# Context and x tokens out of step in the second block of a two-block fp32 kernel

## The chip, the cores and the metric

One core of one Trainium2 chip runs the whole program. The metric is the device time of one execution in microseconds.

## What is computed

Two transformer blocks run one after the other on 256 tokens of width 1024, all in float32. The first block is attention with spatial gating and a mixture of 32 experts. The second block has two layers, in which the 256 tokens of x and 256 tokens of a context run through the same weights; the context can be read by x's attention, and the last layer needs of the context only its keys and values. Cut to what matters:

```python
def swiglu(h, w_gu, w_down):
    g, u = jnp.split(h @ w_gu, 2, axis=-1)
    return (jax.nn.silu(g) * u) @ w_down

for layer in range(2):
    last = layer == 1
    mx = jnp.split(jax.nn.silu(c) @ ada_w[layer] + ada_b[layer], 9, axis=-1)
    mc = jnp.split((jax.nn.silu(c_ctx) @ ada_w[layer] + ada_b[layer])[None, :], 9, axis=-1)
    x   = x   + 0.5 * mx[2][:, None] * swiglu(modulate(rms_norm(x),   mx[0], mx[1]), ffn1_gu, ffn1_down)
    ctx = ctx + 0.5 * mc[2][:, None] * swiglu(modulate(rms_norm(ctx), mc[0], mc[1]), ffn1_gu, ffn1_down)
    hx, hc = modulate(rms_norm(x), mx[3], mx[4]), modulate(rms_norm(ctx), mc[3], mc[4])
    # q, k, v, pool and fourier inputs = h @ w_in; x attends to x and ctx, ctx to ctx
    x = x + mx[5][:, None] * merge_mixers(ax, upx, ufx, ...)      # [attention, pool, fourier] @ w_out
    x = x + 0.5 * mx[8][:, None] * swiglu(modulate(rms_norm(x), mx[6], mx[7]), ffn2_gu, ffn2_down)
    if not last:
        ctx = ctx + mc[5][:, None] * merge_mixers(ac, upc, ufc, ...)
        ctx = ctx + 0.5 * mc[8][:, None] * swiglu(modulate(rms_norm(ctx), mc[6], mc[7]), ffn2_gu, ffn2_down)
return rms_norm(x) * final_gain
```

## The kernel before

**Precision.** Every large product is made of three matmuls (`mm3`, L116 to L118): weights and tokens are each split into a high part and the rest. A weight tile of 512 KB is loaded by SP's queue into `raw`, copied to `whi` by ScalarE (L89), and VectorE subtracts the copy to get `wlo` (L90). There are eight `raw` buffers and four each of `whi` and `wlo`.

**Order.** The code is written as one sequence of tiles, and a scheduler sets the order of the instructions on each engine when the program is built. Each engine then has its own list of instructions.

**The feed-forward** (`ffn`). The hidden width is 22 blocks of 128, taken as 11 pairs. A pair needs four weight tiles for gate and up, and 96 matmuls; in layer 0's FFN2 and layer 1's FFN1 the moving operand has 512 columns, x's 256 tokens beside ctx's 256. Pairs go in groups (0 to 4, 4 to 8, 8 to 11), and a group ends with its down-projection, whose results `gated_add` puts onto x or ctx (L890, L891). Layer 0's FFN1 of ctx is done beside the experts of the first block, ahead of all this.

**A norm** (`norm_hT`, `row_norm`) is a chain over three engines: ScalarE squares and sums a row, VectorE makes the inverse root from small operations (L135 to L146) and the normalised rows `xs` (L160), TensorE transposes them (L122), and ScalarE and VectorE put scale and shift on them and split them into `hT` (L212, L109, L110). Nothing of the next product can start before.

**The mixer** projects keys and values, queries, and the inputs of pool and fourier, for ctx and x in turn; attention, pool and fourier write a copy `cat`. Pool multiplies with a matrix `poolc` for each of four windows, loaded by POOL's queue into one buffer and used for both streams. Then the output projection goes over two halves of the columns, in each half first x's tokens, then ctx's.

**Modulation.** The rows mx and mc of layer 1 are made on VectorE while layer 0 runs: 72 steps, each a load of 512 KB into an `araw` buffer (five of them) and two products with a sum (L840, L841), against two rows of c that also lie in `araw` buffers (`c_rows`, L817). A step comes after every second weight tile (`rate`). The first steps wait, by a copy (L820), for the tile in `self.gate`, the last `hT` of the norm before layer 0's FFN2.

Of the kernel before, what the change touches and what calls it, by code (L numbers as in the profile page):

```python
# [6 lines left out]
F32 = mybir.dt.float32  # L7
# [18 lines left out]
RB = (0,0)  # L26
# [22 lines left out]
W1 = (8,4,4)  # L49
class Builder:  # L50
    def __init__(self, tc, A):
        self.tc, self.nc, self.A = tc, tc.nc, A
        self.side, self.mods = [], {}
        self.rate, self.credit, self.done = 0, 0, 0
        self.gate, self.tanh, self.part, self.turn_ = None, False, {}, 0

# [21 lines left out]
    def W(self, name, idx, cols=1024):  # L78
# [7 lines left out]
        raw = self.t(self.wp, [128, 1024], F32, "raw", self.RAW)  # L86
# [4 lines left out]
        return hi, lo  # L91

# [85 lines left out]
    def norm_hT(self, x, gcol, scol, hh, hl, off, tags=None, ahead=AH):  # L178
# [13 lines left out]
        for kp in range(4):  # L192
# [3 lines left out]
            s = (slice(None), slice(2 * kp, 2 * kp + 2), slice(off, off + 256))  # L196
            if scol is None:
                for kk in range(2):
                    kt = 2 * kp + kk
                    g = gcol[:, kt : kt + 1]  # L200
                    h, l = hh[:, kt, off : off + 256], hl[:, kt, off : off + 256]
# [26 lines left out]
    def build(self, parts=None):  # L228
        tc, nc, A = self.tc, self.nc, self.A
        self.PB = {"mm": 3, "at": 2, "tr": 2, "ada": 1}  # L230
        with tc.tile_pool(name="glob", bufs=1) as G, \
# [11 lines left out]
            with tc.tile_pool(name="keep", bufs=1, reuse_waits="tile") as K:  # L243
# [7 lines left out]
                nc.gpsimd.dma_start(kv, self.ctx)  # L251
            with tc.tile_pool(name="ctxp", bufs=1, reuse_waits="tile") as C:
# [20 lines left out]
    def proj_T(self, p, wb, c, hh, hl, ts, kts=range(8)):  # L273

        for kt in kts:
            wh, wl = wb[kt // 4]
            s = slice((kt % 4) * 256 + c * 128, (kt % 4) * 256 + c * 128 + 128)
            self.mm3(p, (wh[:, s], wl[:, s]), (hh[:, kt, ts], hl[:, kt, ts]), kt == 0, kt == 7)

    def block1(self):  # L280
        tc, nc, A = self.tc, self.nc, self.A
        x = self.x
        T256 = slice(0, 256)
        with tc.tile_pool(name="b1", bufs=1, reuse_waits="tile") as P:
# [4 lines left out]
            self.norm_hT(x, n1g, None, hh, hl, 0, ("tr", "tr", "at", "at"), 4)  # L289
# [58 lines left out]
            for g2 in range(4):  # L348
                wu = [self.W("w_u", 2 * g2 + b) for b in range(2)]
                for c in range(2):  # L350
                    pu = self.mm([128, 256])
                    self.proj_T(pu, wu, c, hh, hl, T256)
# [114 lines left out]
            def merge(br, yT):  # L467
                for d2 in range(4):
                    wg = [self.W("w_gate", br * 8 + 2 * d2 + b) for b in range(2)]
                    wu = [self.W("w_up", br * 8 + 2 * d2 + b) for b in range(2)]  # L470
                    for c in range(2):
                        d = 2 * d2 + c
                        pg = self.mm([128, 256])
                        self.proj_T(pg, wg, c, hh, hl, T256)
# [5 lines left out]
                        self.proj_T(pu, wu, c, yT[:, 0], yT[:, 1], T256)  # L480
# [22 lines left out]
            self.norm_hT(self.ctx, self.seg(mods, 1, 1), self.seg(mods, 1, 0), *self.cT, 0, ("tr",) * 4, 2)  # L503
# [13 lines left out]
    def moe(self):  # L517
        tc, nc, A = self.tc, self.nc, self.A
        x = self.x
        with tc.tile_pool(name="moe", bufs=1, reuse_waits="tile") as P:  # L520
            self.xsp, self.xst = P, ("xg", 6)
            self.gp, self.gpb = P, 1
            ctx_steps = self.ffn(P, 0, 1, ((self.ctx, 0, self.grow(self.mods[0][1], 1, 2)),), self.cT, 256, CUT)
# [129 lines left out]
            def raws(name, idx):  # L653

                out = []
                for n in idx:
                    self.turn_ = (self.turn_ + 1) % (self.RAW + 5)
                    r = self.t(self.wp, [128, 1024], F32, *(("araw", 5) if self.turn_ % 3 == 0 else ("raw", self.RAW)))
# [235 lines left out]
    def ffn(self, P, L, f, streams, hT, n, cuts, first=None):  # L894
# [4 lines left out]
        nb = 2 * max(b - a for a, b in zip(cuts, cuts[1:])) + 2  # L899
        for c0, c1 in zip(cuts, cuts[1:]):  # L900
            hid = []
            for j in range(c0, c1):
                pgu = [[self.mm([128, n], tag) for c in range(2)] for tag in ("mm", "at")]

                parts = [slice(off, off + 256) for _, off, _ in streams] if j == 0 and len(streams) > 1 else [slice(0, n)]
                parts = parts if first is None else parts[::first]
                if len(parts) > 1:
                    wb = [[self.W(gu, (L, o + 2 * j + b)) for b in range(2)] for o in (0, 22)]
                    for ts in parts:
                        for w in range(2):  # L910
                            for c in range(2):
                                self.proj_T(pgu[w][c][:, ts], wb[w], c, *hT, ts)
                else:
                    for w in range(2):
                        for b in range(2):
                            wt = self.W(gu, (L, 22 * w + 2 * j + b))
                            for c in range(2):
                                self.proj_T(pgu[w][c], [wt, wt], c, *hT, parts[0], range(4 * b, 4 * b + 4))
                for c in range(2):
                    s = self.t(P, [128, n], F32, "silu", 2)  # L920
                    fh = self.t(P, [128, n], F32R, "fh", nb)
                    fl = self.t(P, [128, n], F32R, "fl", nb)
# [13 lines left out]
            for c in range(2):  # L936
                out = [(x, off, g, tt) for x, off, g in streams for tt in range(2)]
# [9 lines left out]
                for p, (x, off, g, tt) in zip(ps, out):  # L947
                    self.gated_add(p, g, x, tt, c)
                    if c1 == cuts[-1] and c == 0 and first is not None:
                        self.half(x, tt)  # L950
# [3 lines left out]
    def mixer(self, L, mods, d2, last, hT):  # L954
        nc, tc, A = self.nc, self.tc, self.A
        x, ctx = self.x, self.ctx
        sc, sx = ("c", ctx, 256, 1), ("x", x, 0, 0)
        streams = (sx, sc) if last else (sc, sx)
        full = (sx,) if last else (sc, sx)
        for _, xx, off, a in streams if last else (sx,):  # L960
            self.norm_hT(xx, self.seg(mods, a, 4), self.seg(mods, a, 3), hT[:, 0], hT[:, 1], off)
        with tc.tile_pool(name="mix", bufs=1, reuse_waits="tile") as P:
# [30 lines left out]
            def proj(wb, ncol, stream, ev):  # L993
                kper = 8 // len(wb)
                nm, xx, off, a = stream
                for tt in range(2):
                    p = self.mm([128, ncol])
                    ts = slice(off + tt * 128, off + tt * 128 + 128)
                    for kt in range(8):
                        wh, wl = wb[kt // kper]  # L1000
                        s = slice(kt % kper * ncol, kt % kper * ncol + ncol)
                        self.mm3(p, (hT[:, 0, kt, ts], hT[:, 1, kt, ts]), (wh[:, s], wl[:, s]), kt == 0, kt == 7)
# [86 lines left out]
            cat = self.t(self.B, [128, 2, 8, 512], F32R, "hT")  # L1089

            def attention(stream):
# [3 lines left out]
                for tt in range(2):  # L1095
# [28 lines left out]
                    ts = slice(off + tt * 128, off + tt * 128 + 128)  # L1124
                    self.split(p, cat[:, 0, 0:4, ts], cat[:, 1, 0:4, ts])
# [279 lines left out]
```

## Time and profile before

| | |
|---|---|
| time, median of 3 runs | 2228.83 us (2227.14 to 2238.33) |
| profiled execution | 2229.63 us, span 2227.8 us |
| TensorE busy | 2106.4 us, 95% of the span |
| VectorE, ScalarE busy | 1298.9 us (58%), 838.4 us (38%) |
| mean clock granted to TensorE | 0.979 of full speed |
| DMA | 437.95 MB, 197 GB/s over the span |

A matmul's busy time overlaps the next one's, so busy TensorE is read by the gaps it leaves and by its clock. The second block begins at about 870 us and runs to the end.

### The profile page before, as it was taken

The page shows a single profiled execution, that of the slowest core. Times are in us where ns is not written, and L with a number is a line of the kernel's source. Part 1 is how long each engine was busy: PE and PEld are TensorE (multiplying, and loading weights), DVE is VectorE, ACT ScalarE, POOL GpSimd, SP SyncE. Part 2 cuts the span into 40 slices and gives each one's busy share as a digit, 9 for nine tenths or more (in the row PEclk, how much of TensorE's full clock was granted, in tenths as well). Part 3 has the DMA queues.
Part 4 walks back from the last instruction along what each step waited for, and adds up shares of the span by engine and source line. Part 5 has one row for each costly group of instructions (what it writes and reads, how often), then busy time and mean ns, then how long its engine had stood idle before and what let it go on. Part 6 is the DMA issues. An engine that isn't in the chain of part 4 may idle for free. (4 is left out here: it accounts for less than half of the span.)

```text
span 2227.8 us, 31222 instructions
## 1 busy us (share of the span) xinstructions
PE 2106.4 (95%) x12146; PEld 1695.5 (76%) x12146; DVE 1298.9 (58%) x2311; ACT 838.4 (38%) x1322; POOL 55.4 (2%) x105
## 2 busy tenths in 40 slices
PE   7999999999996999999989999999999999898998
PEld 5888797446464888888778888878888887677997
DVE  5778575223236455685589434998843344856655
ACT  5556453222233444455342222223222223545443
POOL 1000000000001000000000000000000000000000
PEclk9999999999997999999999999998999999899999
DMA  8655656999997867731266323665622223305552
GB/s 314 207 167 172 236 197 243 395 381 416 402 416 264 297 236 284 248 105 43 77 209 215 96 94 121 210 199 163 214 95 95 91 96 99 121 27 161 190 187 78
DMA packets 121207, 437.95 MB, mean 197 GB/s; under 512 B 14352, under 2 KB 14496, under 8 KB 120928
## 3 DMA queue, kind: packets, MB, share of 16 engines
q1 hardware_dynamic: 113760, 413.19, 52.4%
q0 software_dynamic: 7296, 22.74, 3.1%
q8 instruction: 96, 1.57, 0.3%
q14 instruction: 55, 0.45, 0.1%
HBM read 429.53 MB, written 6.34 MB: 196 GB/s over the span
## 5 line engine op out<-in xcount | busy, mean ns | idle before, releaser
L90 DVE TENSOR_TENSOR wlo<-raw,whi 128x1024 fp32r<-128x1024 f32 x448 | 546.8, 1223 | 509.7 <-ACT whi L89 502.8
L89 ACT ACTIVATE whi<-raw 128x1024 fp32r<-128x1024 f32 x448 | 473.9, 1060 | 730.8 <-PE at L117 177.9
L117 PE MATMUL mm<-hT,whi 128*128 128x256 f32 (+1 forms) x736 | 246.2, 336 | 3.1 <-DVE hT L110 2.8
L116 PE MATMUL mm<-hT,whi 128*128 128x256 f32 (+1 forms) x736 | 243.7, 337 | 3.6 <-ACT hT L109 3.6
L118 PE MATMUL mm<-hT,wlo 128*128 128x256 f32 (+1 forms) x736 | 245.1, 334 | 0.6 <-DVE wlo L90 0.6
L117 PE MATMUL at<-hT,whi 128*128 128x256 f32 (+1 forms) x736 | 244.5, 333 | 0.0
L118 PE MATMUL at<-hT,wlo 128*128 128x256 f32 (+1 forms) x736 | 243.9, 333 | 0.0
L116 PE MATMUL at<-hT,whi 128*128 128x256 f32 (+1 forms) x736 | 241.6, 333 | 0.0
L116 PE MATMUL mm<-whi,fh 128*128 128x512 f32 x440 | 172.1, 398 | 5.6 <-ACT whi L89 5.6
L117 PE MATMUL mm<-wlo,fh 128*128 128x512 f32 x440 | 175.0, 399 | 1.6 <-DVE wlo L90 1.6
L118 PE MATMUL mm<-whi,fl 128*128 128x512 f32 x440 | 173.7, 397 | 0.0
L117 PEld LDWEIGHTS mm<-hT,whi 128*128 128x128 f32 x736 | 140.8, 191 | 21.0 <-DVE hT L110 5.4
L116 PEld LDWEIGHTS mm<-hT,whi 128*128 128x128 f32 x736 | 138.9, 191 | 21.1 <-ACT hT L109 5.2
L118 PEld LDWEIGHTS mm<-hT,wlo 128*128 128x128 f32 x736 | 140.8, 191 | 16.4 <-DVE wlo L90 1.0
L117 PEld LDWEIGHTS at<-hT,whi 128*128 128x128 f32 x736 | 140.2, 191 | 16.4 <-issue 1.7
L116 PEld LDWEIGHTS at<-hT,whi 128*128 128x128 f32 x736 | 138.6, 191 | 17.2 <-ACT whi L89 1.7
L118 PEld LDWEIGHTS at<-hT,wlo 128*128 128x128 f32 x736 | 140.2, 190 | 14.7
L116 PEld LDWEIGHTS mm<-whi,fh 128*128 128x128 f32 x440 | 82.6, 189 | 32.9 <-ACT whi L89 11.2
L117 PEld LDWEIGHTS mm<-wlo,fh 128*128 128x128 f32 x440 | 82.9, 188 | 29.3 <-DVE wlo L90 4.6
L932 DVE TENSOR_TENSOR silu<-silu,at 128x256 f32<-128x256 f32 (+1 forms) x104 | 55.2, 531 | 82.4 <-PE at L118 82.1
L118 PEld LDWEIGHTS mm<-whi,fl 128*128 128x128 f32 x440 | 83.0, 189 | 19.1
L116 PE MATMUL mm<-whi,hT 128*128 128x512 f32 (+1 forms) x256 | 95.0, 377 | 2.6 <-ACT hT L109 2.5
(381 smaller groups left out, 3940.6 us busy)
## 6 DMA issues: line engine op xcount, KB each, us to landing
raw<-gu SPq DMA_DIRECT2D x220, 512.0 KB, 4.3
araw<-ada_w SPq DMA_DIRECT2D x144, 512.0 KB, 4.5
raw<-w SPq DMA_DIRECT2D x119, 512.0 KB, 10.0
raw<-dn SPq DMA_DIRECT2D x110, 512.0 KB, 4.2
araw<-w SPq DMA_DIRECT2D x73, 512.0 KB, 10.0
raw<-w_in SPq DMA_DIRECT2D x54, 512.0 KB, 4.2
raw<-w_out SPq DMA_DIRECT2D x24, 512.0 KB, 3.8
raw<-w_gate SPq DMA_DIRECT2D x16, 512.0 KB, 3.4
```

What stands on the lines that cost most here:

```text
L89: self.nc.scalar.activation(out=hi[:, :cols], in_=src, func=AF.Copy)
L90: self.nc.vector.tensor_tensor(out=lo[:, :cols], in0=src, in1=hi[:, :cols].bitcast(F32), op=OP.subtract)
L116: mm(p, lh, rh, start=first, stop=False)
L117: mm(p, lh, rl, start=False, stop=False)
L118: mm(p, ll, rh, start=False, stop=last)
L932: nc.vector.tensor_tensor(out=s, in0=s, in1=pgu[1][c], op=OP.mult)
```

## The change

In the second block the two streams no longer go through the same pairs at the same time.
- FFN2 of layer 0: pairs 0 to 3 of ctx are computed alone beside and after attention of x in the mixer; x's pairs 0 to 3 alone follow the mixer; pairs 3 to 6 and 6 to 9 take both streams; then 9 to 11 of x alone, and of ctx alone, the latter beside x's norm for layer 1.
- FFN1 of layer 1: pairs 0 to 2 of x, 2 to 6 and 6 to 9 of both, 9 to 11 of x; then 0 to 2 of ctx beside x's norm for the mixer, and 9 to 11 of ctx beside the queries of x in the mixer, then ctx's norm.
- A pair alone has matmuls of 256 columns, with tiles of its own (`lsilu`, `lfh`, `lfl`).
- In the mixer the output projection is a function per stream. In layer 0 ctx's comes before attention of x, x's at the end. Pool runs per stream, with its own loads of the matrices. In layer 1 the projection of ctx's keys and values is moved behind queries and pool/fourier inputs of x.
- `hT` is one tile for both streams that lives through the block, attention writes into it, and `cat` goes. `self.gate` is now ctx's half of it, as ctx's norm before FFN2 leaves it.
- `raw` has four buffers; in the first block and the experts four more (`rawk`) take every other load.

```diff
-W1 = (8,4,4)
+W1 = (4,4,4)
+CA = (0, 3)
+EC = (3, 6, 9, 11)
+FC = (2, 6, 9, 11)
...
+    def raw(self):
+        self.rawn += 1
+        if self.K is not None and self.rawn % 2:
+            return self.t(self.K, [128, 1024], F32, "rawk", 4)
+        return self.t(self.wp, [128, 1024], F32, "raw", self.RAW)
...
-    def ffn(self, P, L, f, streams, hT, n, cuts, first=None):
+    def ffn(self, P, L, f, parts, cuts, pre="", ends=()):
...
-        for c0, c1 in zip(cuts, cuts[1:]):
+        for streams, c0, c1 in zip(parts, cuts, cuts[1:]):
+            n = 256 * len(streams)
+            act = streams[0][2] if len(streams) == 1 else self.both
...
-            def pool():
+            def pool(stream):
+                nm, xx, off, a = stream
                 for j in range(2):
-                    ps = [self.mm([128, 256]) for _ in full]
+                    p = self.mm([128, 256])
                     for g2 in range(2):
                         g = 2 * j + g2
                         pP = self.load(P, "c_pool", [128, 2, 256], "poolc", idx=g, bufs=MC)
...
+            def out(stream):
+                nm, xx, off, a = stream
+                g = self.grow(d2, a, 5)
+                for c in range(2):
+                    ps = [self.mm([128, 512]) for _ in range(2)]
+                    for b in range(4):
+                        wh, wl = self.W("w_out2", (L, 4 * c + b))
+                        for tt, p in enumerate(ps):
...
             if last:
                 kx, kc = keys(sx), keys(sc)
                 run(proj(wkv, 256, sx, ev_kv))
                 next(kx)
-                run(proj(wkv, 256, sc, ev_kv))
+                run(proj(weights(2, 4), 512, sx, ev_q), kx)
+                run(queries(sx), side(), n=1)
+                run(proj(weights(6, 4), 512, sx, ev_pf))
+                run(proj(weights(0, 2), 256, sc, ev_kv))
                 next(kc)
-                run(proj(weights(2, 4), 512, sx, ev_q), kx)
-                run(proj(weights(6, 4), 512, sx, ev_pf), kc, queries(sx))
-                run(attention(sx), *((pool(), fourier(sx)) if ORD else (fourier(sx), pool())), n=NF)
+                run(kc, pool(sx))
+                run(attention(sx), fourier(sx), n=NF)
...
-                run(chain(attention(sc), kx, qx), proj(wpf, 512, sc, ev_pf), proj(wpf, 512, sx, ev_pf), n=NA)
-                run(attention(sx), *((pool(), fourier(sc), fourier(sx)) if ORD else (fourier(sc), fourier(sx), pool())), n=NF)
...
+                run(chain(attention(sc), kx, qx), proj(wpf, 512, sc, ev_pf), proj(wpf, 512, sx, ev_pf), pool(sc), fourier(sc), n=NA)
+                run(out(sc))
+                run(attention(sx), pool(sx), fourier(sx), side(), n=NF)
+            run(out(sx))
...
+            def alone(L, f, st, a, b, ends=()):
+                return self.ffn(B, L, f, [(st,)], (a, b), "l", ends)
...
+            def side():
+                norm(0, 1, 6)
+                cs.append(stream(0, 1, 6))
+                yield
+                yield from alone(0, 2, cs[0], *CA)
+            self.need(0, 3)
+            self.mixer(0, *self.mods[0], False, side)
+            sc, = cs
+            self.gate = T[:, 1, 1, 7].bitcast(F32)
+            self.rate = RC[0]
+            norm(0, 0, 6)
+            sx = stream(0, 0, 6)
+            ffn(0, 2, [(sx,), (sx, sc), (sx, sc), (sx,)], (0, *EC), (x,))
+            self.need(1, 1)
+            norm(1, 0, 0)
+            run(alone(0, 2, sc, *EC[-2:], (ctx,)))
+            self.rate = RA[1]
+            sx = stream(1, 0, 0)
+            norm(1, 1, 0)
+            sc = stream(1, 1, 0)
+            ffn(1, 1, [(sx,), (sx, sc), (sx, sc), (sx,)], (0, *FC), (x,))
+            self.need(1, 2)
+            norm(1, 0, 3)
+            run(alone(1, 1, sc, 0, FC[0]))
+            def side():
+                yield from alone(1, 1, sc, *FC[-2:], (ctx,))
+                norm(1, 1, 3)
+            self.mixer(1, *self.mods[1], True, side)
+            norm(1, 0, 6)
+            ffn(1, 2, [(stream(1, 0, 6),)] * 3, (0, 4, 8, 11), (x,))
```

What the scheduler makes of it is read from the order of the instructions on an engine. On VectorE, at x's norm after layer 0's mixer, these rows stand one behind the other before the change (`rsv`, `rsy`, `rsh` are the small tiles of the inverse root, the first token tile's ending in 81 and 82):

```order
L140 TENSOR_SCALAR rsh_10782<-rsy_10781,rsv_10780 128x1
L890 TENSOR_TENSOR gadd<-mm,grow 128x512
L146 SCALAR_TENSOR_TENSOR rsy_10781<-rsh_10782,rsy_10781 128x1
L891 TENSOR_TENSOR x<-x,gadd 128x512
L140 TENSOR_SCALAR rsh_10782<-rsy_10781,rsv_10780 128x1
L146 SCALAR_TENSOR_TENSOR rsy_10781<-rsh_10782,rsy_10781 128x1
L140 TENSOR_SCALAR rsh_10782<-rsy_10781,rsv_10780 128x1
L135 TENSOR_SCALAR rsv_10795<-ss,ssp 128x1
L146 SCALAR_TENSOR_TENSOR rsy_10781<-rsh_10782,rsy_10781 128x1
L136 TENSOR_SCALAR rsy_10796<-rsv_10795 128x1
L160 TENSOR_SCALAR xs<-x,rsy_10781 128x1024
```

And the same norm after it (`rsy_11435` is the first token tile's; L853 and L854 are the two products of a step of layer 1's modulation):

```order
L903 TENSOR_TENSOR gadd<-mm,grow 128x512
L146 TENSOR_SCALAR rsv_11434<-ss,ssp 128x1
L854 SCALAR_TENSOR_TENSOR araw,acols<-araw 128x1024
L904 TENSOR_TENSOR x<-x,gadd 128x512
L147 TENSOR_SCALAR rsy_11435<-rsv_11434 128x1
L853 SCALAR_TENSOR_TENSOR araw,acols<-araw 128x1024
L151 TENSOR_SCALAR rsh_11436<-rsy_11435,rsv_11434 128x1
L146 TENSOR_SCALAR rsv_11449<-ss,ssp 128x1
L854 SCALAR_TENSOR_TENSOR araw,acols<-araw 128x1024
L157 SCALAR_TENSOR_TENSOR rsy_11435<-rsh_11436,rsy_11435 128x1
L147 TENSOR_SCALAR rsy_11450<-rsv_11449 128x1
L151 TENSOR_SCALAR rsh_11436<-rsy_11435,rsv_11434 128x1
```

The small operations of both versions are the same; products of 1024 columns now stand among them, up to the normalised rows and behind them, where before there was none ahead of the gate's copy.

On TensorE, at the end of layer 0's FFN2, the last rows of the down-projection (`fh`, `fl`) run straight into the transposes of x's norm before the change:

```order
L116 MATMUL at<-whi,fh 128x512
L117 MATMUL at<-wlo,fh 128x512
L118 MATMUL at<-whi,fl 128x512
L122 MATMUL tr<-ident,xs 128x128 x12
L116 MATMUL mm<-hT,whi 128x256 x2
L116 MATMUL at<-hT,whi 128x256 x2
```

After it, the down-projection of x's last two pairs is followed by matmuls of 256 columns of ctx's last two pairs, and x's transposes stand further on among those:

```order
L129 MATMUL mm<-whi,fl 128x512
L127 MATMUL mm<-whi,fh 128x512
L128 MATMUL mm<-wlo,fh 128x512
L129 MATMUL mm<-whi,fl 128x512
L127 MATMUL mm<-hT,whi 128x256
L128 MATMUL mm<-hT,whi 128x256
L129 MATMUL mm<-hT,wlo 128x256
```

What moved is ctx's share of the last two pairs: out of the 512-column matmuls ahead of the norm, to 256-column matmuls beside it.

## Rows read from the trace of the kernel before

**Rows 1.** The page: busy time of each engine, and one group of weight loads.
```profile
PE 2106.4 (95%) x12146; PEld 1695.5 (76%) x12146; DVE 1298.9 (58%) x2311; ACT 838.4 (38%) x1322; POOL 55.4 (2%) x105
...
L117 PEld LDWEIGHTS mm<-hT,whi 128*128 128x128 f32 x736 | 140.8, 191 | 21.0 <-DVE hT L110 5.4
```

**Rows 2.** Windows: length, then busy time (instructions) of each engine, clock, DMA share, GB/s.
```profile
975.00:1075.00 100.00, 97.04 (x623) 81.02 (x622) 57.33 (x146) 51.11 (x130) 2.43 (x5) 1.00 0.18 56
1075.00:1100.00 25.00, 25.00 (x113) 20.30 (x112) 10.69 (x17) 6.56 (x11) 1.60 (x3) 1.00 0.36 128
1100.00:1150.00 50.00, 44.13 (x280) 37.66 (x278) 40.67 (x88) 21.25 (x34) 2.10 (x4) 1.00 0.46 158
1150.00:1200.00 50.00, 49.77 (x222) 40.50 (x223) 47.27 (x72) 18.16 (x23) 0.00 (x0) 1.00 0.68 222
...
1475.00:1550.00 75.00, 65.74 (x357) 56.60 (x357) 64.74 (x134) 26.65 (x47) 2.08 (x4) 0.89 0.47 155
...
1875.00:1925.00 50.00, 37.85 (x200) 31.51 (x199) 32.56 (x95) 18.19 (x38) 5.85 (x11) 0.86 0.29 88
1925.00:1975.00 50.00, 44.87 (x228) 34.30 (x226) 37.73 (x105) 29.61 (x62) 2.77 (x7) 0.93 0.38 121
1975.00:2050.00 75.00, 65.87 (x427) 58.14 (x427) 43.25 (x75) 35.15 (x63) 0.54 (x1) 0.93 0.27 88
```

**Rows 3.** Waits of TensorE, 870 to 2227 us: sum, times, longest.
```profile
PE tr L122 <- DVE xs L160: 20.4, 6, 8.8
...
PE mm L1136 <- DMA poolc<-c_pool: 5.6, 2, 4.1
```

**Rows 4.** Timeline at x's norm before layer 1's FFN2: start, length, instruction.
```profile
2020.08 0.40 PE L118 MATMUL mm<-whi,hT 128*128 128x512 f32 x1
...
2021.40 0.68 DVE L890 TENSOR_TENSOR gadd<-mm,grow 128x512 f32<-128x512 f32 x1
...
2022.00 1.22 DVE L90 TENSOR_TENSOR wlo<-raw,whi 128x1024 fp32r<-128x1024 f32 x1
...
2023.14 0.21 DVE L135 TENSOR_SCALAR rsv<-ss,ssp 128x1 f32<-128x1 f32 x1
...
2024.35 0.16 DVE L146 SCALAR_TENSOR_TENSOR rsy<-rsh,rsy 128x1 f32<-128x1 f32 x1
...
2024.54 0.27 DVE L140 TENSOR_SCALAR rsh<-rsy,rsv 128x1 f32<-128x1 f32 x1
...
2027.28 0.75 DVE L160 TENSOR_SCALAR xs<-x,rsy 128x1024 f32<-128x1024 f32 x1
...
2030.84 0.56 PE L116 MATMUL mm<-hT,whi 128*128 128x256 f32 x1
```

**Rows 5.** Timeline of VectorE after layer 0's mixer.
```profile
1106.15 0.75 DVE L160 TENSOR_SCALAR xs<-x,rsy 128x1024 f32<-128x1024 f32 x1
...
1129.80 1.23 DVE L840 SCALAR_TENSOR_TENSOR araw<-araw 128x1024 f32<-128x1024 f32 x1
```

**Rows 6.** Timeline of TensorE: first and last of 16 and of 49 matmuls.
```profile
1885.71 0.39 PE L118 MATMUL mm<-whi,fl 128*128 128x512 f32 x1
...
1889.21 0.40 PE L118 MATMUL at<-whi,fl 128*128 128x512 f32 x1
...
2060.50 0.28 PE L116 MATMUL at<-hT,whi 128*128 128x256 f32 x1
...
2066.13 0.28 PE L116 MATMUL mm<-hT,whi 128*128 128x256 f32 x1
```

**Rows 7.** VectorE's groups, 1150 to 1200 us: busy, mean ns, idle before.
```profile
L840 DVE SCALAR_TENSOR_TENSOR araw<-araw 128x1024 f32<-128x1024 f32 x12 | 14.6, 1220 | 2.5 <-DMA araw<-ada_w 2.5
L90 DVE TENSOR_TENSOR wlo<-raw,whi 128x1024 fp32r<-128x1024 f32 x10 | 12.1, 1218 | 0.1
```

**Rows 8.** The page's DMA issues: count, size, median us to landing.
```profile
araw<-ada_w SPq DMA_DIRECT2D x144, 512.0 KB, 4.5
...
araw<-w SPq DMA_DIRECT2D x73, 512.0 KB, 10.0
```

More of the change, by code (lines that the diff above doesn't have):

```diff
@@ L176, in half, with norm_hT @@
         nc.vector.tensor_scalar(out=ss, in0=ss, scalar1=1024 * EPS, scalar2=None, op0=OP.add)
-    def norm_hT(self, x, gcol, scol, hh, hl, off, tags=None, ahead=AH):
+    def norm_hT(self, x, gcol, scol, hh, hl, tags=None, ahead=AH):
         tags = tags or TG
@@ L656, in raws @@
                 for n in idx:
[L657 to L658 removed]
+                    self.turn_ += 1
+                    r = self.t(self.wp, [128, 1024], F32, "araw", 5) if self.turn_ % 3 == 0 else self.raw()
                     nc.sync.dma_start(r, A[name][n])
@@ L901, in ffn @@
             hid = []
             for j in range(c0, c1):
[L903 to L912, printed above, removed]
-                else:
[L914 to L918, printed above, removed]
+                if pre:
+                    pp = [self.mm([128, 2, 256]) for c in range(2)]
+                    pgu = [[pp[c][:, w] for c in range(2)] for w in range(2)]
+                else:
+                    pgu = [[self.mm([128, n], tag) for c in range(2)] for tag in ("mm", "at")]
@@ L936, in ffn @@
             for c in range(2):
-                out = [(x, off, g, tt) for x, off, g in streams for tt in range(2)]
+                out = [(x, 256 * i, g, tt) for i, (x, g, _) in enumerate(streams) for tt in range(2)]
                 ps = [self.mm([128, 512], tag) for tag in ("mm", "mm", "at", "at")[: len(out)]]
@@ L948, in ffn, with mixer @@
                     self.gated_add(p, g, x, tt, c)
-                    if c1 == cuts[-1] and c == 0 and first is not None:
+                    if c1 == cuts[-1] and c == 0 and any(x is e for e in ends):
                         self.half(x, tt)
                     yield
-    def mixer(self, L, mods, d2, last, hT):
+    def mixer(self, L, mods, d2, last, side):
         nc, tc, A = self.nc, self.tc, self.A
         x, ctx = self.x, self.ctx
+        T = self.T
         sc, sx = ("c", ctx, 256, 1), ("x", x, 0, 0)
@@ new lines, in block2, with norm, stream, run @@
+            T = self.T = self.t(B, [128, 2, 2, 8, 256], F32R, "hT")
+            def norm(L, a, s):
+                mods = self.mods[L][0]
+                self.norm_hT((x, ctx)[a], self.seg(mods, a, s + 1), self.seg(mods, a, s), T[:, a, 0], T[:, a, 1])
+            def stream(L, a, s):
+                return (x, ctx)[a], self.grow(self.mods[L][1], a, s + 2), self.one(a)
+            def run(steps):
+                for _ in steps:
+                    pass
+            def ffn(L, f, parts, cuts, ends=()):
+                with tc.tile_pool(name="ffn", bufs=1, reuse_waits="tile") as P:
+                    run(self.ffn(P, L, f, parts, cuts, ends=ends))
@@ new lines, in alone @@
+            def alone(L, f, st, a, b, ends=()):
+                return self.ffn(B, L, f, [(st,)], (a, b), "l", ends)
+            self.need(0, 1)
+            self.rate = RA[0]
+            norm(0, 0, 0)
+            ffn(0, 1, [(stream(0, 0, 0),)] * 3, (0, 4, 8, 11), (x,))
+            self.dbg("f1x0", x)
+            self.need(0, 2)
+            self.rate = RB[0]
+            norm(0, 1, 3)
+            norm(0, 0, 3)
+            cs = []
+            def side():
+                norm(0, 1, 6)
+                cs.append(stream(0, 1, 6))
+                yield
+                yield from alone(0, 2, cs[0], *CA)
```

152 lines of the change are left out of this document (61 added, 91 removed).

## The prediction

> **What bounds the kernel now.** The first view is the profile's page: TensorE is busy 2106.4 of 2227.8 us, VectorE 58%, ScalarE 38% [rows 1]. So the time is TensorE's work, its clock, and the places where it stands still. The profiled execution took 2229.63 us, 0.8 above the median of 2228.83 and 1.8 above its span; the sum below is made against 2229.63.
>
> I then cut the second block into windows and looked for stretches with TensorE idle or a granted clock below 1 [rows 2]. Lost time is idle time plus (1 - clock) x length; idle time inside a half-clock stretch is counted slightly twice by this, so it is an upper figure.
> - 975 to 1075, attention of layer 0: 2.96 us.
> - 1100 to 1150, x's norm after layer 0's mixer: 5.87.
> - 1475 to 1550, the norms before layer 1's FFN1: 9.26 idle + 0.11 x 75 = 17.5.
> - 1875 to 1925, the norms before layer 1's mixer: 12.15 + 7.0 = 19.2.
> - 1925 to 1975, inside that mixer: 5.13 + 3.5 = 8.6.
> - 1975 to 2050, its end and x's norm before FFN2: 9.13 + 5.25 = 14.4.
>
> The sum is 68.5 us. The list of waits says what ends the stops: transposes (L122) waiting for the normalised rows xs (L160), 20.4 us in six stops, the longest 8.8; and a pool matrix, one of 4.1 us [rows 3]. An uncovered norm reads like this [rows 4]: the last matmul ends at 2020.48, the gated additions and small dependent operations follow, the second xs starts at 2027.28 and takes 0.75, and the next FFN matmul starts at 2030.84. That is 10.4 us: 7.6 to the end of the second xs and 2.8 from there on. After layer 0's mixer the same norm costs less, because in each half of the out-projection x's tokens come first and ctx's matmuls then cover x's norm: the second xs of x starts at 1106.15, and VectorE begins the products of layer 1's modulation (L840, L841) only at 1129.80, right after the copy that waits for the gate (L820) [rows 5].
>
> **The change, term by term.**
>
> *Matmuls.* Seven FFN pairs run per token stream instead of over both: 7 x 96 = 672 matmuls of 512 columns become 1344 of 256. From 2060.50 to 2066.13 there are 48 steps of 256 columns, 0.1173 us each; from 1885.71 to 1889.21 there are 15 steps of 512, 0.2333 each [rows 6]. So 672 x (2 x 0.1173 - 0.2333) = +0.9 us. The Trainium skill ("TensorE: Matmul & The Clock Gate", section "Back-to-back issue gap") speaks against such a split: it gives some 81 ns for a matmul of 128 columns in a sustained stream and 131 ns for 512, so that halving a matmul saves much less than half. With 98 ns for 256 by a straight line between the two, an estimate from that page, the term would be 672 x 65 ns = +44 us. This trace disagrees, with 233 ns at 512 and 117 at 256.
>
> *Weights.* 64 more tiles are loaded and split: 64 x 1.22 us [rows 7] = 78 us on VectorE, which is free 42% of the program. Beside TensorE-bound pairs this is hidden; where VectorE is full it is part of the next term.
>
> *From layer 0's attention to its FFN2.* Three things move together: ctx's out-projection goes ahead of attention of x, ctx's first three FFN2 pairs stand ahead of x's out-projection, and the gate now hangs on ctx's norm, not x's. So the products start before x's out-projection, and VectorE's order (shown above) has them between the operations of x's norm, which no half of ctx covers any more.
>  - Beside the ctx pairs, from their second weight tile to the last one of x's out-projection, VectorE has 26 products and 20 weight splits at 1.15 us start to start (2022.00 to 2023.14 in [rows 4]), 11 operations of 512 columns at 0.60 (2021.40 to 2022.00) and 12 of 256 at about 0.35, an estimate from these: 63.5 us. TensorE has 178 matmuls of 256 and 158 of 512 columns: 57.7. VectorE is slower by 5.8 us, and not ahead when the norm comes.
>  - From the last split for x's out-projection to the end of the second xs VectorE has 17 products (19.6 us), 4 splits (4.6), 7 operations of 512 columns (4.2), 18 small ones at 0.19 (3.4; 2024.35 to 2024.54 in [rows 4]) and two xs (1.4): 33.2 us. TensorE's part of that is 12 matmuls, 2.8 us; I take off 3 more for a split done ahead. So 27.4 us of standstill, 2.8 to the first matmul as in [rows 4], and 2 for two products between the operations on the transposes: 32 us. Lower bound: VectorE ahead by its four buffers of split weights, 12 x 0.2333 x 4 = 11 us instead of 3: 24. Upper bound: no head start, and products that wait for their loads as now, 2.5 us per 50 [rows 7]: 37.
>  - After a stop the clock is at half for a while. The stop of 8.8 us [rows 3] goes with 0.14 x 50 = 7 us of clock [rows 2], much of it inside the stop itself; I take 3.
>  - Together 5.8 + 32 + 3 = 40.8 where 5.9 were lost: +35 us.
>
> *Layer 0 to layer 1, and layer 1's FFN1 to its mixer.* x finishes first, and two ctx pairs alone stand behind it: 192 x 0.1173 + 48 x 0.2333 = 33.7 us of matmuls over a norm chain of 10.4. TensorE's order (shown above) has them between x's last down-projection and x's transposes, and VectorE's has no product among the operations of these two norms. VectorE's work there is 12 splits (13.8), the norm (7) and gated additions with the hidden layer (8): 29 of 33.7 us, so the chain is done in time. I leave 3 us at each for the interlocking of transposes and hT: 6 - 17.5 - 19.2 = -30.7 us; bounds -36.7 (nothing left) and -20 (VectorE late by 5 us at each).
>
> *Pool matrices.* Each stream now loads its own: 12 loads instead of 8, through one buffer; an exposed one costs 4.1 us [rows 3]. In POOL's queue the two c_rows loads (now L830), which wait for araw buffers, stand among them instead of behind them all. Attention of each stream covers layer 0's; I take +2 (0 to 4 x 4.1 = 16). In layer 1, pool of x stands beside the keys of ctx with three loads in a row, the copies of ctx's keys (now L1071) behind them in POOL's queue, and little matmul work between; but ctx's last FFN1 pairs now cover the queries of x. I take 0 (-4 to +8).
>
> *The rest.* Layer 1's mixer to FFN2 (14.4), the last norm and layer 0's FFN1 stay. In the first block and the mixture of experts eight raw buffers become 4 and 4 in another pool: 0, at most a late load or two of 4.5 us [rows 8].
>
> Sum: 0.9 + 35 - 30.7 + 2 = +7; I forecast 2236 us. What two transitions gain is spent at a third.
>
> **The rivals.**
>  1. *Faster: VectorE has room at layer 0's transition.* If it comes to x's norm four splits ahead, the standstill is 24 instead of 32, the 5.8 us beside the ctx pairs vanish, and the pool loads are hidden: 2236 - 8 - 5.8 - 2 = 2220, and with nothing left at the two covered norms 2214. For it: VectorE is busy only 10.69 of 25 us ahead of that place, from 1075 on [rows 2]. Against it: the count of 63.5 against 57.7 us, and VectorE's 47.27 of 50 beside the same products, from 1150 on [rows 2]. Chance 0.28.
>  2. *Slower: the products wait for their loads.* Five araw buffers hold two rows of c and, per step, a load and a product's output, so three rotate: a load is issued when the first product of the step two before is done. At a landing of 4.5 us [rows 8] a step then takes (4.5 + 1.15) / 2 = 2.8 us; the transition leaves 33.2 / 8.5 = 3.9 for one, so nothing waits. From a landing of 2 x 3.9 - 1.15 = 6.6 us on it does. At the 10.0 of loads in the busiest stretch [rows 8] a step takes 5.6: the 8.5 steps 14 us longer, the 13 steps ahead of them 9, 2236 + 23 = 2259. Weights behind a waiting load in SP's queue would wait too. Chance 0.20.
>  3. *Slower: the pool matrices.* If four loads of layer 0 expose 4.1 us each and two of layer 1 as well, 2236 - 2 + 25 = 2259. Chance 0.11.
>  4. *Slower: a matmul of 256 columns can't hide its weight load.* A load takes 191 ns [rows 1]; at that pace the term is 672 x (2 x 0.191 - 0.2333) = 100 us, 2335. The Trainium skill's figures above point the same way. Against it: the 48 steps of [rows 6] are this very kind of matmul. Chance 0.01.
>
> That the change doesn't cover layer 1's norms at all would cost 30.7 more; the orders say otherwise, and I put it into rival 4's hundredth.
>
> **How the numbers follow.** The forecast has 0.40, rival 1 0.28, the others 0.32. A measurement of this kernel tells about 0.5%, 11 us, from no change: the forecast lies within that, rival 1 mostly on the fast side (below 2218), the others beyond 2240. So faster 0.27, same 0.40, slower 0.33. The range goes from below rival 1's 2214 by another 5 us (bound -36.7 and the -4 of layer 1's pool) to rivals 2 and 3: 2209 to 2260; the forecast's own range is 2224 to 2246.
>
> **What would show it.** In the profile after, TensorE's longest stop should stand behind x's out-projection in layer 0, 20 us or more, ended by xs, with products (now L853, L854) among the norm's operations on VectorE; the losses before layer 1's FFN1 and before its mixer should fall from 37 to about 6 us, with the clock at 1. I am wrong if that first stop is under 15 us (then faster), if VectorE waits for ada_w loads by 10 us or more there, if poolc ends over 10 us of TensorE's waits, or if 256-column matmuls step by more than 0.12 us.

## The result, and the profile after

The changed kernel takes 2255.86 us (median of 4, 2254.91 to 2265.01), the kernel before 2229.66 on the same chips. The ratio is 1.012, with a 95% interval of 1.0082 to 1.0158: 26 us slower. The forecast was 2236, no change, with a range of 2209 to 2260; the time lies in the range, and it is the case "slower", which had 0.33.

The page of the changed kernel, span and busy time of the engines; compare [rows 1]:

```profile
span 2254.6 us, 33045 instructions
...
PE 2105.7 (93%) x12818; PEld 1726.8 (77%) x12818; DVE 1393.9 (62%) x2443; ACT 915.7 (41%) x1426; POOL 58.4 (3%) x109
```

The matmuls take as long as before, 2105.7 us against 2106.4. The span is 26.8 us longer, and TensorE's time outside matmuls went from 121.4 to 148.9, by 27.5. So the change is read as standstill. Windows like those of [rows 2], moved to where each stage now stands and cut a little wider: length, busy time of TensorE, weight loads, VectorE, ScalarE and POOL, granted clock, DMA share, GB/s.

```profile
375.00:650.00 275.00, 243.20 (x1581) 150.85 (x1584) 80.81 (x103) 71.04 (x104) 6.49 (x12) 0.96 0.98 391
925.00:1125.00 200.00, 192.23 (x1120) 155.09 (x1119) 136.37 (x336) 112.40 (x229) 12.05 (x24) 0.97 0.38 124
1125.00:1250.00 125.00, 93.23 (x585) 82.24 (x584) 116.96 (x196) 45.13 (x65) 1.57 (x3) 0.88 0.71 233
1500.00:1575.00 75.00, 74.60 (x533) 68.81 (x532) 60.34 (x112) 44.34 (x71) 2.08 (x4) 1.00 0.62 201
1850.00:1900.00 50.00, 49.09 (x334) 44.37 (x333) 40.21 (x70) 27.98 (x47) 2.88 (x6) 1.00 0.66 202
1950.00:2075.00 125.00, 105.80 (x625) 88.76 (x625) 72.37 (x146) 60.25 (x117) 3.49 (x7) 0.90 0.28 88
```

Of the kernel before, the experts, layer 0's mixer up to x's norm, and layer 1's mixer up to FFN2, which [rows 2] don't show in these cuts:

```profile
375.00:650.00 275.00, 254.11 (x1626) 150.99 (x1626) 82.59 (x104) 72.91 (x107) 7.04 (x13) 0.99 1.00 402
...
925.00:1100.00 175.00, 172.04 (x1019) 142.57 (x1019) 111.23 (x291) 88.32 (x201) 8.75 (x17) 1.00 0.28 94
...
1925.00:2050.00 125.00, 110.74 (x652) 92.45 (x651) 80.99 (x179) 64.76 (x124) 3.31 (x8) 0.93 0.31 101
```

| stage | TensorE idle before | after | clock before | after |
|---|---|---|---|---|
| experts, 375 to 650 | 20.9 | 31.8 | 0.99 | 0.96 |
| layer 0's mixer, up to x's norm | 3.0 | 7.8 | 1.00 | 0.97 |
| x's norm before FFN2, layer 0 (after: and the ctx pairs) | 5.9 | 31.8 | 1.00 | 0.88 |
| norms before layer 1's FFN1 | 9.3 | 0.4 | 0.89 | 1.00 |
| norms before layer 1's mixer | 12.2 | 0.9 | 0.86 | 1.00 |
| layer 1's mixer and x's norm before FFN2 | 14.3 | 19.2 | 0.93 | 0.90 |

Both halves of the forecast can be seen. Two norms are covered and their low clock is gone; a third stands open for 25 us. What the forecast did not have is in the first, second and last row. The six rows together have 26.3 us more of idle time, nearly all of the 27.5. TensorE's waits, 870 us to the end, against [rows 3]:

```profile
PE tr L133 <- DVE xs L171: 37.0, 5, 24.9
PE mm L127 <- DVE gadd L903: 5.1, 7, 1.8
PE tr L133 <- ACT e L1124: 4.9, 3, 2.6
...
PE mm L1154 <- DMA poolc<-c_pool: 3.7, 2, 3.4
```

The stop of 24.9 us and what VectorE does in it, line by line:

```profile
1191.35 0.39 PE L129 MATMUL mm<-whi,hT 128*128 128x512 f32 x1
1216.64 1.12 PE L133 MATMUL tr<-ident,xs 128*128 128x128 f32 x4 [24.90 <-DVE xs L171]
```

```profile
1204.41 0.20 DVE L146 TENSOR_SCALAR rsv<-ss,ssp 128x1 f32<-128x1 f32 x1
1204.53 1.22 DVE L854 SCALAR_TENSOR_TENSOR araw<-araw 128x1024 f32<-128x1024 f32 x1
...
1205.67 0.69 DVE L904 TENSOR_TENSOR x<-x,gadd 128x512 f32<-128x512 f32 x1
1206.28 0.15 DVE L147 TENSOR_SCALAR rsy<-rsv 128x1 int32<-128x1 int32 x1
1206.34 1.22 DVE L853 SCALAR_TENSOR_TENSOR araw<-araw 128x1024 f32<-128x1024 f32 x1
...
1207.48 0.27 DVE L151 TENSOR_SCALAR rsh<-rsy,rsv 128x1 f32<-128x1 f32 x1
1207.67 0.20 DVE L146 TENSOR_SCALAR rsv<-ss,ssp 128x1 f32<-128x1 f32 x1
1207.79 1.22 DVE L854 SCALAR_TENSOR_TENSOR araw<-araw 128x1024 f32<-128x1024 f32 x1
...
1208.93 0.16 DVE L157 SCALAR_TENSOR_TENSOR rsy<-rsh,rsy 128x1 f32<-128x1 f32 x1
...
1219.09 0.75 DVE L171 TENSOR_SCALAR xs<-x,rsy 128x1024 f32<-128x1024 f32 x1
```

A product (L853 or L854, 1.22 us) stands after every one to four of the small operations of 0.15 to 0.3 us. From the first of them (L146, 1204.41) to the end of the second xs it is 15.4 us; in [rows 4] the same stretch of an uncovered norm, from 2023.14 on, took 4.9. The rest of the stop lies ahead of it: when the matmuls end, at 1191.7, VectorE is behind, and until 1204.4 it works off products, two weight splits and gated additions.

### The profile page after: what moved, and what is told of

It reads as the page before. It is cut to its first block, busy times and chain, and to the rows that moved or that the text cites. A ratio compares the mean times of both kernels' runs of the same rounds, so it can differ in the third digit from the quotient of the medians.

```text
span 2254.6 us, 33045 instructions
## 1 busy us (share of the span) xinstructions
PE 2105.7 (93%) x12818; PEld 1726.8 (77%) x12818; DVE 1393.9 (62%) x2443; ACT 915.7 (41%) x1426; POOL 58.4 (3%) x109
## 4 chain that ended last, share of the span: by engine, by line
PE 46%; DVE 3%; issue 2%; DMA 1%; ACT 1%; DVEq 0%; ACTq 0%; POOLq 0%; POOL 0%
PE mm L127 9%; PE mm L128 9%; PE mm L129 9%; PE at L127 5%; PE at L129 5%; PE at L128 5%; PE tr L133 1%; PE ada L1134 1%; DVE wlo L94 1%; DMA araw<-ada_w 1%; DVE araw L854 1%; DVE araw L853 0%; DMA poolc<-c_pool 0%; PE at L1120 0%; DVE gadd L903 0%
## 5 line engine op out<-in xcount | busy, mean ns | idle before, releaser
L94 DVE TENSOR_TENSOR wlo<-raw,whi 128x1024 fp32r<-128x1024 f32 x440 | 538.1, 1224 | 375.0 <-ACT whi L93 369.9
L128 PE MATMUL mm<-hT,whi 128*128 128x256 f32 (+1 forms) x992 | 302.6, 306 | 0.7 <-DVE hT L121 0.7
L127 PE MATMUL mm<-hT,whi 128*128 128x256 f32 (+1 forms) x992 | 301.8, 308 | 1.5 <-DVE gadd L903 1.1
L129 PE MATMUL mm<-hT,wlo 128*128 128x256 f32 (+1 forms) x992 | 301.1, 306 | 0.0
L128 PE MATMUL at<-hT,whi 128*128 128x256 f32 (+1 forms) x704 | 221.4, 315 | 0.0
L127 PE MATMUL at<-hT,whi 128*128 128x256 f32 (+1 forms) x704 | 220.8, 316 | 0.0
L129 PE MATMUL at<-hT,wlo 128*128 128x256 f32 (+1 forms) x704 | 220.5, 315 | 0.0
L127 PEld LDWEIGHTS mm<-hT,whi 128*128 128x128 f32 x992 | 186.3, 189 | 14.4 <-DVE gadd L903 1.6
L128 PEld LDWEIGHTS mm<-hT,whi 128*128 128x128 f32 x992 | 187.6, 189 | 11.2 <-DVE hT L121 1.3
L129 PEld LDWEIGHTS mm<-hT,wlo 128*128 128x128 f32 x992 | 187.1, 189 | 10.4 <-issue 0.8
L127 PEld LDWEIGHTS at<-hT,whi 128*128 128x128 f32 x704 | 132.4, 189 | 12.5 <-ACT whi L93 1.4
L128 PEld LDWEIGHTS at<-hT,whi 128*128 128x128 f32 x704 | 132.9, 189 | 9.5
L94 DVE TENSOR_TENSOR wlo<-rawk,whi 128x1024 fp32r<-128x1024 f32 x72 | 88.1, 1224 | 71.7 <-ACT whi L93 69.9
L93 ACT ACTIVATE whi<-rawk 128x1024 fp32r<-128x1024 f32 x72 | 76.2, 1058 | 93.3 <-PE mm L129 37.9
```

The costliest lines, as they stand in the source:

```text
L93: self.nc.scalar.activation(out=hi[:, :cols], in_=src, func=AF.Copy)
L94: self.nc.vector.tensor_tensor(out=lo[:, :cols], in0=src, in1=hi[:, :cols].bitcast(F32), op=OP.subtract)
L127: mm(p, lh, rh, start=first, stop=False)
L128: mm(p, lh, rl, start=False, stop=False)
L129: mm(p, ll, rh, start=False, stop=last)
```

## The experiments

Three theories were told apart. **Products:** the products in VectorE's list make the stop, and cost what it costs. **Fullness:** VectorE has too much to do up to layer 1 wherever the products stand. **Elsewhere:** the loss comes from other parts of the change, the raw buffers, the pool matrices or the order of the mixers.

**e1: the gate alone.**

```diff
-            self.gate = T[:, 1, 1, 7].bitcast(F32)
             self.rate = RC[0]
             norm(0, 0, 6)
+            self.gate = T[:, 0, 1, 7].bitcast(F32)
```

> The changed kernel with one line moved: the gate of layer 1's modulation hangs on x's norm before layer 0's FFN2 again, not on ctx's. If the products among the operations of that norm make the stop of 24.9 us, it falls to that of an uncovered norm, 6 to 8 us, the waits of the ctx pairs on gated additions go too, and the time is about 20 us below the changed kernel's 2256: 2232 to 2240. Rival: VectorE has too much work up to layer 1 wherever the products stand; then the time moves by less than 8 us, 2248 or more, and new waits for weights appear in layer 0's FFN2.

Measured 2264.77 us, 1.0165 (1.0144 to 1.0185): no gain over the change itself, and 9 us more by the medians (the intervals of the two ratios just overlap). The stop did fall, to 6.2 us, and x's transposes began at 1193.9 instead of 1216.6. But it was lost again before layer 1, as the windows of e1 show:

```profile
1175.00:1225.00 50.00, 42.40 (x277) 38.81 (x276) 38.74 (x69) 22.73 (x35) 0.54 (x1) 0.90 0.52 171
1450.00:1600.00 150.00, 130.09 (x800) 113.19 (x800) 141.69 (x247) 61.27 (x92) 2.09 (x4) 0.93 0.71 228
```

From 1450 to 1600 TensorE is idle for 19.9 us, with VectorE busy for 141.7 of 150. The second third of the modulation, which ran right after the first in the changed kernel, now fell on x's and ctx's last pairs alone, and the last third began among layer 1's first norms. The expectation failed; the rival was right about the time, but not about the reason, as e13 shows.

**e2: cover for the norm instead.** The line `yield from alone(0, 2, cs[0], *CA)` in the mixer's `side` becomes `run(alone(0, 2, sc, *CA))` behind `norm(0, 0, 6)`.

> The changed kernel with ctx's first three FFN2 pairs moved: x's norm comes first and these pairs follow it in the code, so that 50.6 us of matmuls stand beside the norm; the gate stays on ctx's norm, so products still stand before and among the norm's operations. If the missing cover is what makes the stop, nearly all of it goes: 25 to 30 us below 2256, 2226 to 2231. Rival: products ahead of the weight splits starve the pairs as well, VectorE being full; then the stop is only divided up among waits for weights, 2240 or more.

Measured 2295.55 us, 1.0298 (1.0275 to 1.0322), 40 us slower than the change. The stop is divided up into many, among the ctx pairs from 1202 on and again from 1515 to 1625 beside the last pairs alone and layer 1's norms. The rival was right.

**n: both kernels without the products.**

```diff
-                nc.vector.scalar_tensor_tensor(out=jk, in0=raw, ..., in1=cb[1], ..., accum_out=cols[:, 1, n : n + 1])
-                nc.vector.scalar_tensor_tensor(out=raw, in0=raw, ..., in1=cb[0], ..., accum_out=cols[:, 0, n : n + 1])
```

> The kernel before without the 144 products of layer 1's modulation on VectorE; their loads stay, and layer 1 runs on wrong modulation, which changes no duration. If the products of the kernel before are hidden beside pairs of both streams, it gains little, 3 to 9 us, where products stand next to the norms before layer 1's FFN1: 2221 to 2227. Rival: VectorE's work costs time there too; then 2215 or less.

> The changed kernel without these products, in the same way. What it takes less than the changed kernel is what the products cost there; what it takes less than the kernel before without them is what the change is worth apart from them. If the products in the list make the stop of 24.9 us, that stop is 6 to 8 us here and the time is 2230 to 2236, and the rest of the change about breaks even (two covered norms against raw buffers, attention of layer 0, layer 1's mixer). Rival: the products are the whole of the loss; then 2210 or less. Second rival: they only fill a stop that is there anyway; then above 2245.

Measured 2220.62 (0.9951, 0.9931 to 0.9972) and 2243.91 (1.0055, 1.0037 to 1.0073). Without the products layer 1's modulation is not computed, so these two runs are only good for time. The products cost the kernel before some 10 us, a little more than expected, and the changed one 12. Its stop is 6.6 us here, as expected; its time is not, 8 us above the expected range and just under the second rival's 2245. This reading is clouded: without the products the scheduler also put the last part of attention of x among the first ctx pairs, and the stretch from the mixer's first transposes to x's norm takes 264.5 us, against 252.2 in e13, which has the products. So the pair says that the change loses without products too, not how much.

**e13: the steps handed out.** e1, and the modulation kept off every norm and, as far as possible, off the pairs alone:

```diff
-RC = (.5,0)
+RC = (.72,0)
...
+            self.rate = 0
             run(alone(0, 2, sc, *EC[-2:], (ctx,)))
...
             norm(1, 1, 0)
+            self.gate = T[:, 1, 1, 7].bitcast(F32)
```

> The changed kernel with the gate on x's norm as in e1 and the steps handed out so that none falls on a norm or beside a pair alone where it can be helped: 0.72 steps per weight tile in layer 0's FFN2 instead of 0.5, none beside ctx's last pairs alone, and the last third gated by ctx's norm of layer 1. If what e1 lost again before layer 1 came from its second third beside pairs alone, both stops are gone: 2230 to 2238. Rival: VectorE is full in layer 0's FFN2 whatever the order, and the loss only moves on: 2245 or more.

Measured 2228.98 us, 0.9992 (0.9976 to 1.0009): as fast as the kernel before, so fullness falls: the same 144 products cost 27 us less in other places. The reading offered is room per weight tile. Beside a pair of both streams a tile gives TensorE 24 matmuls of 512 columns, 5.6 us; beside a pair alone it gives 24 of 256, 2.8 us, while VectorE's split of the tile takes 1.22 both times. It is not a bar on products beside pairs alone, as two windows show, e13's, mostly beside x's first pairs alone, and e1's, beside last pairs alone:

```profile
1200.00:1240.00 40.00, 40.00 (x294) 37.79 (x294) 37.31 (x58) 19.41 (x28) 0.00 (x0) 1.00 0.81 266
```

```profile
1460.00:1480.00 20.00, 14.89 (x107) 14.07 (x105) 19.29 (x31) 6.46 (x8) 0.00 (x0) 0.91 0.77 260
```

In the first VectorE has 15 products in 40 us and TensorE never stops; in the second it has 9 in 20 and TensorE is idle for 5.1. Which of the repairs in e13 gave how much was not separated.

**f1: the gate put back, with all else repaired.** e15 (below) with the edit of e1 undone.

> The kernel of e15 with one thing of the change put back: the gate of layer 1's modulation on ctx's norm in layer 0's mixer. Products then stand again before and among the operations of x's norm, and nothing else on the way to layer 1 moves onto a norm. If these products make the stop, it comes back with 24 to 26 us instead of 6.2, and the time is 18 to 25 us above e15's 2223: 2241 to 2248. Rival: what they take here the emptier list gives back later; then under 8 us, 2231 or less.

Measured 2244.47 us (1.0058, 1.0036 to 1.0079), 21.2 above e15. x's transposes in layer 0, first f1's, then e15's:

```profile
1202.29 1.09 PE L133 MATMUL tr<-ident,xs 128*128 128x128 f32 x4 [24.71 <-DVE xs L171]
```

```profile
1175.88 1.09 PE L133 MATMUL tr<-ident,xs 128*128 128x128 f32 x4 [6.24 <-DVE xs L171]
```

The stop is back, 24.7 us instead of 6.2, and little else moves: the mixer begins at 926.0 against 926.3, the way from these transposes to layer 1's first is 313.1 us against 315.1, and from there to the end 727.7 against 726.4. This is the price of the gate.

**e4: the raw buffers alone.** The kernel before with `W1 = (4,4,4)`, `rawk`, and the experts' turn as changed.

> The kernel before with the change of the raw buffers alone: four and four others in the first block and the experts, four in the second block. If this is why the experts end some 5 us later in the changed kernel, the time is 2233 to 2236 and the experts' TensorE waits for ScalarE's copies rise from 7 to about 14 us. Rival: the experts end later for another reason (the order of the ctx pairs and modulation beside them); then it stays at 2229 to 2231.

Measured 2236.65 us, 1.0031 (1.0018 to 1.0044): 6.8 us. The experts' waits of TensorE, first in the kernel before, then in e4:

```profile
PE at L692 <- DMA raw<-w: 5.7, 15, 1.4
PE mm L116 <- ACT whi L89: 5.4, 7, 1.7
```

```profile
PE mm L124 <- ACT whi L90: 11.8, 7, 2.6
...
PE at L701 <- DMA raw<-w: 5.9, 8, 2.0
PE at L701 <- DMA rawk<-w: 4.5, 9, 1.1
```

The waits for ScalarE's copies double, as expected. In the profiled executions only about half of the loss stands ahead of layer 0's mixer, whose first transposes begin at 936.1 instead of 932.6; some 3 us more are lost from there to x's norm, where this kernel too has four raw buffers.

**e14: the turn of the buffers.** e13 with

```diff
-                    self.turn_ += 1
+                    self.turn_ = (self.turn_ + 1) % 13
```

> The kernel of e13 with the even turn of the buffers for the experts alone. If it is the uneven turn that cost the experts 5 us and more, layer 0's FFN1 begins about 10 us earlier than in e13 and the time is e15's within 4 us, 2220 to 2227; then holding back the rows of c is worth next to nothing. Rival: holding them back gave e15's gain: 2228 or more.

Measured 2217.83 us, 0.994 (0.9918 to 0.9961): 11 us below e13 and faster than both kernels. The number of buffers, 13 with `araw`, is that of e4 and of the kernel before. Only the share of loads differs: one third to each of the three kinds in the changed kernel (64 to `araw` with five buffers, 65 to `rawk` and 63 to `raw` with four each), against 5 in 13 to `araw` now. The same waits in e14:

```profile
PE mm L127 <- ACT whi L93: 5.4, 6, 1.7
PE at L705 <- DMA raw<-w: 2.6, 7, 1.1
PE at L705 <- DMA rawk<-w: 2.1, 6, 0.7
```

TensorE is busy for 255.85 us from 375 to 650 here, 242.74 in e13. The mixer's first transposes in the kernel before, in e13 and in e14:

```profile
932.56 0.66 PE L122 MATMUL tr<-ident,xs 128*128 128x128 f32 x4
```

```profile
936.53 1.09 PE L133 MATMUL tr<-ident,xs 128*128 128x128 f32 x8
```

```profile
925.84 1.09 PE L133 MATMUL tr<-ident,xs 128*128 128x128 f32 x8
```

The gain is made ahead of the mixer, by the turn and not by the number of buffers. It is more than the change had lost there, 4.0 us (936.6 in the changed kernel); why e14 is ahead of the kernel before at this place stays open.

**e5 and e15: the rows of c.** In short, `nc.vector.tensor_copy(cb[a][:, 0:1], gate[:, 0:1])` ahead of each load of `c_rows`, in the changed kernel and in e14.

> The changed kernel with the loads of the two rows of c held back, by a copy of one column from the gate's tile into each, until ctx's norm is done. In the changed kernel their Silu falls between the exponentials of both attentions of layer 0 and ScalarE loads its tables four times more, 1.28 us each. If that and the half clock behind it are a part of layer 0's mixer's loss, the stops of 1.2 and 2.6 us in the softmax go and the time falls by 4 to 9 us, to 2247 to 2252. Rival: the pool matrices and the order of the mixer cost this; then 2254 to 2258.

> The last kernel with two more repairs: the experts' loads go round 13 buffers evenly again (5, 4 and 4) instead of a third to each kind, and the two rows of c are held back until the gate opens, so that no Silu stands among the exponentials. If the raw buffers cost 5 us by their uneven turn and the tables 6, it is 8 to 12 us below the last kernel, 2220 to 2228. Rival: four buffers of a kind are too few in any order, and the mixer's gain is lost later as it was in e5: within 3 us of the last kernel.

What it is about, ScalarE and then TensorE in the changed kernel:

```profile
1067.27 1.28 ACT L1124 ACT_TABLE_LOAD   x1
1068.56 0.69 ACT L1124 ACTIVATE e<-at,nm 128x512 f32<-128x512 f32 x1
```

```profile
1069.39 0.66 PE L133 MATMUL tr<-ident,e 128*128 128x128 f32 x4 [2.60 <-ACT e L1124]
```

A table load stands ahead of an exponential because the Silu of `c_rows` came before it; twelve such loads in the program instead of eight. The Trainium skill ("ScalarE activation tables: per-element evaluation and per-set limits", section "What a function is on this engine") gives 1283 ns for one. The trace agrees, with 1283 ns on average. Measured: e5 2257.65 us (1.0126, 1.0105 to 1.0146), no gain. The stops in the softmax went, and from the mixer's first transposes to x's norm it is 6.1 us shorter (939.0 to 1212.9 against 936.6 to 1216.6 in the changed kernel), but 3.6 were lost up to layer 1 and 2.4 had been lost earlier. e15 took 2223.24 us (0.9967, 0.9951 to 0.9982), 5.7 below e13, but 5.4 above e14 (the intervals of the two ratios just overlap). So e15's gain over e13 is the turn's; what holding the rows back gives in the mixer is gone by layer 1, in e15 with a weight split that comes 3.2 us late beside the products.

**f2: layer 1's mixer.**

```diff
-                run(proj(weights(2, 4), 512, sx, ev_q), kx)
-                run(queries(sx), side(), n=1)
-                run(proj(weights(6, 4), 512, sx, ev_pf))
+                run(side(), kx)
+                run(proj(weights(2, 4), 512, sx, ev_q))
+                run(proj(weights(6, 4), 512, sx, ev_pf), queries(sx))
```

> The kernel of e15 with layer 1's mixer in another order: ctx's last FFN1 pairs alone come before the queries of x, so that 22 us of projections instead of 11 follow ctx's norm, and the queries' chain runs beside the pool and fourier projection. If the stop of 3.1 us at ctx's norm and the half clock behind it are an uncovered norm, they go: 4 to 7 us below e15, 2216 to 2220. Rival: the queries' chain or the pool matrices take their place: 2221 or more.

Measured 2222.58 us (0.9959, 0.9944 to 0.9974), as e15. The waits of TensorE in this mixer, e15's first, then f2's:

```profile
PE mm L1155 <- DMA poolc<-c_pool: 3.5, 2, 3.2
PE tr L133 <- DVE xs L171: 3.4, 1, 3.4
```

```profile
PE mm L1155 <- DMA poolc<-c_pool: 6.7, 3, 4.4
```

The norm's stop is gone, and the pool matrices take its place: three loads through one buffer, one behind the other. The rival was right. Two buffers for them were not tried.

**f5: e2's cover, without products near it.** f2 with ctx's pairs as in e2, and 0.56 steps per tile.

> The kernel of f2 with ctx's first three FFN2 pairs behind x's norm in the code, as in e2, but with the gate on x's norm and 0.56 steps per weight tile, so that no product stands near that norm. If e2's loss of 40 us came from the products beside the pairs alone and at the norms before layer 1, covering the norm now gains the 6.2 us of its stop and half clock: 5 to 10 us below f2, 2208 to 2214. Rival: attention of x needs these pairs as its own cover; then f2's time or more, with new stops in the softmax.

Measured 2228.97 us (0.9987, 0.9974 to 1.0), 6 above f2; the rival was right. The norm is covered, but the pairs are missing in attention of x, where stops of up to 2.0 us and a low clock appear. A wait from 1090 to 1260, and a window of attention with a clock of 0.60 (f2, whose attention ends at 1102, has 1.00 from 1080 to 1100):

```profile
PE tr L133 <- ACT hft L223: 2.9, 2, 2.0
```

```profile
1100.00:1120.00 20.00, 14.65 (x67) 12.56 (x66) 7.15 (x13) 6.76 (x13) 0.00 (x0) 0.60 0.00 0
```

## Why the prediction was half right, point by point

- **The stop behind x's out-projection.** Right, in place, cause and size: 27.4 us of standstill were worked out to the second xs, 24.9 and 2.1 were measured, ended by xs, with the 17 products that were counted. Of the 5.8 us beside the ctx pairs (their terms add up to 63.7, not 63.5) some 3.6 came, as idle time from 1125 to the stop. VectorE waited for ada_w loads for 2.5 us from 1125 to 1225, under the 10 at which the prediction called itself wrong, so rival 2 did not happen. f1 shows the gate to be the cause, with 21.2 us. By the prediction's measure, idle time and clock, this stage lost 46.8 us instead of 5.9: 41 more where 35 were forecast, and an upper figure, since much of the low clock lies inside the stop.
- **The two covered norms.** Right: -30.7 was forecast. By the same measure 36.7 us became 1.3, with idle time down from 21.4 to 1.3 and the clock at 1.
- **The matmuls.** Right: the busy time did not change, and 256-column matmuls still step by 0.117 us (1235.23 to 1238.87, 31 steps), so the split costs nothing that can be seen. The estimate from the Trainium skill's figures for a sustained stream ("TensorE: Matmul & The Clock Gate", section "Back-to-back issue gap") was 44 us; no row shows that.
- **"In the first block and the mixture of experts eight raw buffers become 4 and 4 in another pool: 0, at most a late load or two of 4.5 us."** This step failed: the sum had 0 for it. In the changed kernel layer 0's mixer begins 4.0 us late; the raw buffers alone cost 6.8 (e4), in many short waits of at most 2.6 us and not in a late load or two; and the even turn gives 11 (e14), more than was lost. The forecast counted the buffers and not the share of loads that goes through each kind. The experts run at the pace of their loads (DMA busy 98% of the time or more, 402 GB/s before, 391 after, 403 in e14), so a worse turn shows at once; that a share after the number of buffers is the best one was not tested.
- **Pool matrices, +2 and 0.** The size was off and the cause was another. In layer 0's mixer 4.8 us more of idle time, and a clock of 0.97, were measured; poolc ends only 3.7 us of all waits. Two of the stops, 1.2 and 2.6 us, stand behind table loads; that the rows of c would be loaded among the exponentials was seen in POOL's queue, but not what their Silu does on ScalarE. A third piece of the low clock, 0.86 from 925 to 950, stands at the mixer's first transposes, ahead of these table loads, and has no cause shown. In layer 1's mixer it is 4.9 more of idle time and 0.03 of clock: ctx's norm is covered by 11 us of projection where it needs a little more, and then the pool matrices wait (f2).
- **Rival 1** (VectorE four splits ahead) did not happen: VectorE was busy for 117.0 of the 125 us from 1125 on, and the stop came out as counted.
- **The sum.** +7 forecast, +26 measured. Of the 19 us between them 4 to 7 are the experts; some 5 each, an estimate from the idle time, are the two mixers, with a part of their clock. The split of the mixers' loss among table loads, pool matrices, order and the four raw buffers is not settled: the runs that took one away shifted another.
- **The range.** That the time lies in it is in part luck. Its slow end came from rivals 2 and 3, and neither happened; the forecast's own range ended at 2246.

## What to carry to other kernels

A tile that gates background work decides which list it stands in: before moving it, count what will stand between the operations of the next dependent chain, and price the chain by that sum. Count the room for background work per weight tile: a stage cut in two halves doubles the other engines' share per tile. When buffers are shared out to streams of loads, look at the share of loads that goes to each kind beside its number of buffers; here that was worth 11 us.

## What was not expected

- One statement in the order of use of 13 buffers was worth 11 us (e13 to e14), where the forecast had 0, and made the fastest version, 2217.83 us.
- The scheduler's answer to a small edit is not local. e1 moved one line, gained 22.7 us at its place and lost over 30 later; taking the products out moved a part of attention of x.
- Stops of 1.2 and 2.6 us in the softmax each went with a short stretch at the half clock (0.93 over 25 us in two windows of layer 0's mixer), where the kernel before had 1.00 in every window of that mixer.
